# A two-layer encoder trunk on one core: spreading matmuls, roots and partial sums placed at other points of the output stages

## The chip, the cores and the metric

The kernel runs on one core of a Trainium2 chip. The metric is the device time of one execution in microseconds (us), the median of several executions. The engines are TensorE (PE in the rows, PEld its weight loads), VectorE (DVE), ScalarE (ACT), GpSimd (POOL) and SyncE (SP), which issues nearly all DMA transfers.

## The reference, cut to what matters

Two layers, 2048 tokens, width 1024, float32. Each layer ends in the same way, and only this end is touched:

```python
h = h + (o * jax.nn.silu(z)) @ w_out                       # "front" products
gate = jax.nn.sigmoid(rms_norm(h, ple_norm_g[i]) @ ple_w_gate[i])   # "back" products
h = h + (p[i] @ ple_w[i]) * gate
...
return rms_norm(h, final_norm_g)                           # after the second layer
```

`o` is the attention output before its division by the softmax denominator, `z` the gate path, and `p[i] @ ple_w[i]` is computed ahead and lies in DRAM (`ple`).

## The kernel before

All activations are kept transposed (features on the partitions, tokens along the row), 512 tokens to a group `tg` (four groups). Every float32 operand is cut into a high and a low part, so one 128x1024 by 1024x512 product is 24 matmuls (helper `mm3`, lines 290 to 292).

**Order.** `Plan` collects steps with a due time and emits them sorted; PE, ACT, DVE and POOL execute in exactly that order, each engine in its own queue. The order of the DMA issues on SP isn't bound to the plan: the compiler places them itself. Due times inside the output stage count in units in which one 512-column product has `UNIT` = 5.19; `u` below is such a unit (about 1.05 us), and `8U` is one group (41.52 u).

**The output stage** is class `Post`, scheduled once after the first layer (Post 0) and once after the second (Post 1, `final`), each with 32 front products, then 32 back products (in Post 1 the last group is two half groups of 256 columns, called 3 and 4).

- Front, group `tg`: `front` (8 blocks f), `add` the residual (DVE, L812), `x_square` (ACT, L827), `gather` (POOL, L833: partial sums of squares), `x_load` and `x_store` (SP, L804, L818) over a ring of three buffers `xrs`.
- Operands of the next group, c = 0 to 7: `o_load` (SP, L734 `of`, L737 `zt`; three buffer pairs `duos`), `o_spread` (one matmul, L771, that spreads the reciprocal denominators over 64 rows each), `o_gate` (DVE L778, then POOL L779), `o_cut` (ACT L216, DVE L218). Before them, once per group, `spread_load` (SP, L753) and `spread_cut` (ACT L761 twice, DVE L763).
- Sum of a group (`sums_at`): `sum_split` (ACT L216, DVE L218 into blkE), `sum_mm` (two matmuls, L266), `sum_copy`, `sum_out` and `root_in` (DMA out and in), `root` in three steps (DVE L236; ACT square root L240; DVE L244 to L249), `root_out` (DMA, L876, 512 separate floats to `rs`). `SUMS` holds their distances. `row_in` (DMA, L283) later broadcasts `rs` to all partitions; the row scales the back products.
- Back, group g: `h_load` (L887), `h_cut` (ACT L228, DVE L229) for the next group; `back`; `mixin` steps 0 to 4 (DVE L922, ACT L927 sigmoid, POOL L929 gate product, DVE L931, ACT L827); `gather`; `p_load` (L904), `h_store` (L936). In Post 1, `finish` (DVE L940) applies the final norm to a group after its `row_in`; the half groups take their root by `turn` (PE L950, DVE L956, ACT, DVE L249, PE L970) without DRAM, and the last one ends in `finish_last`.

The dense attention ahead of Post 1 ends with `recip` and `store_recip` of its last unit.

Of the kernel before, what the change touches and what calls it, by code (L numbers as in the profile page):

```python
# [18 lines left out]
D = 1024  # L19
T = 2048  # L20
NT = T // P
NC8 = D // P
TG = 512
NG = T // TG
# [8 lines left out]
STLAG, PSLAG = 1.5, 1.19  # L33
US = 1 / 1.3
UNIT = 5.19
PS_X, PS_EV, PS_ST, PS_SS, PS_H, PS_P, PS_HS, PS_SB = 2.17, 0.61, 2.06, 6.29, 1.2, 3, 0.68, 6.5
L_FIRST, L_PACE, L_CUT = -32, 2.6, (9.44, 10.74, 22.24, 26.4, 32.24)
L_US, PS_SL = -0.33, 6.5
A_W1 = ((0, 1), (1, 2), (2, 4), (4, 8))
PREP, PLE_LD = 3, 12  # L40
PS_O1 = 15.5
PS_WL, PS_OL, PS_OL2, PS_HL, PS_R1, PS_R2 = 4, 4, 3.72, 3.96, 2.57, 3
L_LD, L_UL, L_KR, L_VS, L_QS, L_NS = 4, 4, 3, 1.8, 1.8, 1.8
G_WL, G_UL, G_R, G_ST = 4.5, 4.5, 3.5, 2.2
D_S, D_S2 = 0.02, 0.05
D_K0, D_KP, D_KM, D_Q, D_R2, D_V = 0.64, 3.7, 9.5, 8, 27, 19
D_LAT, D_RR, D_W = 19, 20, 21
SUMS = (3, 4.2, 5, 7.5, 10.5, 10.7, 13, 14)
G_W, G_U = (-15.79, -9, 2, 8), -9.81
PL_SUM = (4.5, 5.8, 6.6, 8, 9.5, 10.6)  # L50
VLAG, GATHAT, ACCAT, DENAT, RECIPAT = 4.3, 1.3, 1.4, 8.4, 13.4
KLAG, RLAG, OLAG, DLAG, ILAG = 1, 0.8, 1, 0.8, 0.6
# [79 lines left out]
class Plan:  # L132
# [5 lines left out]
    def add(self, t, f, *args):  # L138
        self.steps.append((t, f, args))
# [537 lines left out]
class Post:  # L677
# [4 lines left out]
    def __init__(self, k, layer, spots, o_dram, rden, z_dram, w_out, resid, out, early):  # L682
        self.k, self.layer, self.final = k, layer, layer == 1
        self.o_dram, self.rden, self.z_dram, self.resid, self.out = o_dram, rden, z_dram, resid, out
        self.srcs = (w_out, k.a["ple_w_gate"][layer])
        w0, w1, self.ospots = spots["w0"], spots["w1"], spots["o"]
        self.wspots = w0, w1 + w0[:4]
        halves = [((blk, kb), (blk, kb + 2)) for spot in w0[4:] for blk, kb in spot]
        self.hspots = self.ospots[0], halves
        self.stages = k.fring(*((4,) * early + (0, 4) * 8))  # L690
        two, rows, baccs = ((36, 38, 40), (30, 32), (28, 34)) if self.final else ((30, 32, 34), (36, 38), (28, 40))
        self.ins = [[("F", kb) for kb in kbs] for kbs in ((8, 10, 12), two if self.final else (0, 2, 14))]
        self.duos = [[("F", kb) for kb in kbs] for kbs in ((8, 10), (12, two[0]), two[1:])]
        self.rdens = k.ring(*(("R", kb) for kb in (88, 90)) if self.final else (("Y", kb) for kb in (8, 10)))
        self.selspot = ("R", 92) if self.final else ("Y", 12)
        self.xrs, self.sqs, self.faccs, self.baccs = k.fring(18, 20, 22), k.fring(26), k.fring(24, 14), k.fring(*baccs)
        self.lasts = k.fring(4, 6)
        self.rows, self.gts, self.plts = k.fring(*rows), k.fring(18, 20, 22), k.fring(26, 14)
        self.spare = ("F", baccs[1])
        first = [("F", kb) for kb in (8, 10, 12, *two, 24, 16)]  # L700
        if self.final:
            self.hfs = first + [("Z", 2 * i) for i in range(16)] + first
        else:
            self.hfs = (first + [("F", kb) for kb in (0, 2, 4, 6)]) * 3
        self.mps, self.sums = k.banks(0, 7), k.banks(7, 8)
        self.w = [[None] * NC8, [None] * NC8]
        self.st = {}
        self.segs = [(0, 512), (512, 512), (1024, 512)] + ([(1536, 256), (1792, 256)] if self.final else [(1536, 512)])
        self.gate_g = k.gam[:, 2 + layer]
# [154 lines left out]

    def root(self, i, g, step):
        if step == 0:
            self.st["root"] = self.k.root_start(self.st["ss"], D, "p")
        elif step == 1:
            self.k.root_table(self.st["root"])
        else:  # L870
            out = self.k.rcol[:, 4 * g : 4 * g + 4] if i == 2 and not self.final else None
            self.st["r"] = self.k.root_end(self.st["root"], out)

    def root_out(self, i, g):
        dst = self.k.rs[self.slot(i)][self.span(i, g)].rearrange("(t p) -> p t", p=P)
        self.k.nc.sync.dma_start(dst, self.st["r"])  # L876

    def row_in(self, i, g):
        sp = self.span(i, g)
# [64 lines left out]
    def turn(self, g, step):  # L944

        k, nc = self.k, self.k.nc
        if step == 0:
            acc = self.st.pop(("acc", 2, g))
            self.st["s"] = self.sums.next()[:, : acc.shape[-1]]
            nc.tensor.matmul(self.st["s"], lhsT=fv(k.ones), rhs=acc, start=True, stop=True)  # L950
        elif step == 1:
            ps = self.st["s"]
            n = ps.shape[-1] // P
            ss, junk = k.small.tile("sp", 4)[:, :n], self.gts.tile([P, P])
            for i in range(n):
                nc.vector.tensor_tensor_reduce(  # L956
                    out=junk, in0=ps[:, i * P : (i + 1) * P], in1=k.ident, scale=1.0, scalar=0.0,
                    op0=ALU.mult, op1=ALU.add, accum_out=ss[:, i : i + 1],
                )
            self.st["root"] = k.root_start(ss, D, "p")  # L960
        elif step == 2:
            k.root_table(self.st["root"])
        elif step == 3:
            self.st["r"] = k.root_end(self.st["root"])
        elif step == 4:
            r = self.st["r"]
            n = r.shape[-1]
            ps = self.mps.next()[:, : n * P]
            for i in range(n):
                nc.tensor.transpose(ps[:, i * P : (i + 1) * P], r[:, i : i + 1].broadcast_to([P, P]), k.ident)  # L970
            self.st["rowp"] = ps
        else:
            row = self.lasts.tile([P, self.st["rowp"].shape[-1]])
            nc.scalar.copy(row, self.st["rowp"])
            self.st["row", 2, g] = row
# [31 lines left out]
    def schedule(self, plan, base, tables):  # L1007
# [5 lines left out]
        for tg in range(NG):  # L1013
            for f in range(NC8):
                t = (NC8 * tg + f) * UNIT
                te = t + UNIT + PS_EV
                add(t, self.front, tg, f)
                add(te - PS_X, self.x_load, tg, f)
                add(te, self.add, tg, f)
                add(te + 0.9, self.x_square, tg, f)  # L1020
                add(te + 1.6, self.gather, 1, tg, f)
                add(te + PS_ST, self.x_store, tg, f)
                if tg > 0:
                    to = NC8 * (tg - 1) * UNIT + (PS_O1 + 3.2 * f if tg == 1 else 4.7 * f + 4)
                    add(to - PS_OL2 - (4.2 if tg > 1 else 3.3), self.o_load, tg, f)
                    add(to - 0.6, self.o_spread, tg, f)
                    add(to, self.o_gate, tg, f, "both")
                    add(to + 1.9, self.o_cut, tg, f, "both")
                    if f == 0:
                        add(to - 7, self.spread_load, tg)  # L1030
                        add(to - 2, self.spread_cut, tg)
            self.sums_at(add, NC8 * (tg + 1) * UNIT + PS_SS, 1, tg)
        t = NG * NC8 * UNIT
        for tg in range(NG):
            tb = t + NC8 * tg * UNIT
            add(tb - (PS_R1 if tg < NG - 1 else PS_R2), self.row_in, 1, tg)
            for f in range(NC8):
                th = tb - NC8 * UNIT + (0.5 + 0.8 * f if tg == 0 else 1.2 + 0.75 * f) * UNIT + PS_H
                add(th - PS_HL, self.h_load, tg, f)
                add(th, self.h_cut, tg, f)  # L1040
        for g, (lo, n) in enumerate(self.segs):
            x, last = n / TG, self.final and g == len(self.segs) - 1
            unit = x * UNIT
            for f in range(NC8):
                te = t + unit + PS_EV
                add(t, self.back, g, f)
                add(te - PS_P, self.p_load, g, f)
                for i, dt in enumerate((0, 0.9, 1.7, 3.2, 4.1) if n == TG else (0, 0.55, 1, 1.9, 2.5)):
                    add(te + dt, self.mixin, g, f, i)
                add(te + (4.9 if n == TG else 3), self.gather, 2, g, f, "vector" if last else "gpsimd")  # L1050
                t += unit
                if not self.final:
                    add(te + 4.2 + PS_HS, self.h_store, g, f)
# [14 lines left out]
                        add(times[5] + 0.8 + f, self.finish, g, f)  # L1068
                        add(times[5] + 1.6 + f, self.h_store, g, f)
            if self.final and n == TG:  # L1070
                fin = t + PS_SB + 20
                add(fin - 3, self.row_in, 2, g)
                for f in range(NC8):
                    add(fin + 1.3 * x * f, self.finish, g, f)
                    add(fin + 1.3 * x * f + 1, self.h_store, g, f)
# [442 lines left out]
class Dense:  # L1518
# [212 lines left out]
    def schedule(self, plan, base):  # L1731

        nu = len(self.units)
        for u, (h, g) in enumerate(self.units):
# [16 lines left out]
            plan.add(t0 + NT + ACCAT, self.split_acc, u)  # L1751
            plan.add(t0 + NT + DENAT, self.density, u)
            plan.add(t0 + NT + DENAT + DLAG, self.spread, u)
            plan.add(t0 + NT + RECIPAT, self.recip, u)
            plan.add(t0 + NT + RECIPAT + ILAG, self.store_recip, u)
            if h % 2 == 1 and h + 1 < HEADS and g < 2:
                for i in range(2):
                    plan.add(t0 + KAT[i] + 0.5, self.k_mm, (h + 1) // 2, 2 * g + i)
# [66 lines left out]
```

## Time and profile before

| | us |
|---|---|
| three runs, median (lowest, highest) | 3672.93 (3672.21, 3678.47) |
| the profiled execution | 3679.53 |
| its span, first to last instruction | 3677.8 |
| mean granted TensorE clock, share of full | 0.985 |
| PE, DVE, ACT, POOL busy, share of the span | 97%, 65%, 62%, 54% |

In the profiled execution the front products of Post 0 begin at 837.55 and its back products at 1047.19; those of Post 1 begin at 3254.53 and 3454.12. A product of 24 matmuls without disturbance takes 5.44 us from start to start (2.88 us with 256 columns), a spreading matmul 0.23, and the two matmuls of a sum 0.45. In a time line, the bracket behind an instruction is the idle time of its engine just before it and what ended it. "Releasers" are inferred from semaphores.

### The profile page before, as it was taken

The numbers are of one execution on the slowest core, as the hardware profiler recorded it, in microseconds if no ns is written. First come the engines' busy times: TensorE is split into PE (matmuls) and PEld (weight loads), VectorE is DVE, ScalarE is ACT, GpSimd is POOL, SyncE is SP. The second block draws the span as 40 slices with busy tenths as digits, with TensorE's granted clock in tenths as the row PEclk, the third lists the DMA queues.
The fourth block names the chain that finished last, engine by engine and source line by source line (L and its number), as shares of the span: only waits on it lengthen the run. The fifth ranks groups of instructions, "written<-read, shape, count | busy, mean of one in ns | idle before, by whom it ended". The sixth has DMA issues, their size and how long they took to land. (4 is left out here: it accounts for less than half of the span.)

```text
span 3677.8 us, 52432 instructions
## 1 busy us (share of the span) xinstructions
PE 3551.2 (97%) x17118; PEld 2967.2 (81%) x17118; DVE 2404.9 (65%) x4539; ACT 2277.0 (62%) x4267; POOL 1973.3 (54%) x1564
## 2 busy tenths in 40 slices
PE   8999999999899899999999999999999999989997
PEld 6888888877787798899888888888888888867776
DVE  6111169995444444514989898989898989964445
ACT  6111279994233433422989898989898989952333
POOL 5331310033333432111989898989898989953243
PEclk9999999999999999999999999999999999999998
DMA  5332378876654676654111212121212121066533
GB/s 189 134 118 89 106 208 203 199 193 200 165 142 133 162 220 220 224 163 131 36 51 35 54 36 59 35 58 36 57 36 58 36 63 36 26 193 178 173 97 106
DMA packets 380080, 428.18 MB, mean 116 GB/s; under 512 B 46287, under 2 KB 233167, under 8 KB 379102
## 3 DMA queue, kind: packets, MB, share of 16 engines
q1 hardware_dynamic: 360798, 390.75, 38.8%
q10 hardware_dynamic: 19008, 34.09, 2.5%
q8 instruction: 134, 2.20, 0.3%
q14 instruction: 140, 1.15, 0.1%
HBM read 251.65 MB, written 156.17 MB: 111 GB/s over the span
## 5 line engine op out<-in xcount | busy, mean ns | idle before, releaser
L1648 POOL TENSOR_TENSOR blkR<-blkF,blkX 128x512 fp32r<-128x512 f32 x1024 | 1351.6, 1333 | 177.8 <-PE ps L1638 51.7
L1609 DVE TENSOR_REDUCE blkF<-ps 128x1 f32<-128x512 f32 x1024 | 700.5, 684 | 77.4 <-PE ps L1605 41.6
L1640 ACT ACTIVATE blkF<-ps 128x512 f32<-128x512 f32 x1024 | 611.4, 597 | 100.1 <-PE ps L1638 51.1
L1641 ACT CAST blkX<-blkF 128x512 fp32r<-128x512 f32 x1024 | 635.5, 621 | 32.8
L1658 DVE TENSOR_TENSOR ps<-ps,blkF 128x512 f32<-128x512 f32 x896 | 615.5, 687 | 0.7
L1669 PE MATMUL ps<-blkR 128*128 128x512 f32 x1024 | 405.4, 396 | 1.1 <-POOL blkR L1648 1.1
L1668 PE MATMUL ps<-blkX,blkR 128*128 128x512 f32 x1024 | 405.2, 396 | 0.0
L290 PE MATMUL ps<-blkR 128*128 128x512 f32 (+2 forms) x888 | 341.2, 384 | 5.6 <-ACT blkR L216 5.4
L291 PE MATMUL ps<-blkR 128*128 128x512 f32 (+2 forms) x888 | 339.2, 382 | 0.6 <-DVE blkR L218 0.6
L292 PE MATMUL ps<-blkR 128*128 128x512 f32 (+2 forms) x888 | 338.9, 382 | 0.3 <-DVE blkR L218 0.3
L833 POOL TENSOR_TENSOR blkF<-blkF 128x512 f32<-128x512 f32 (+1 forms) x112 | 145.8, 1302 | 247.0 <-ACT blkF L827 236.8
L363 DVE TENSOR_TENSOR blkF<-ps,blkF 128x512 f32<-128x512 f32 x72 | 49.5, 691 | 301.4 <-PE ps L292 296.4
L218 POOL TENSOR_TENSOR blkR<-blkF,blkR 128x1024 fp32r<-128x1024 f32 (+1 forms) x39 | 73.5, 1889 | 305.6 <-ACT blkR L216 278.2
L1669 PEld LDWEIGHTS ps<-blkR 128*128 128x128 f32 x1024 | 194.7, 190 | 47.0 <-POOL blkR L1648 2.4
L1668 PEld LDWEIGHTS ps<-blkX,blkR 128*128 128x128 f32 x1024 | 194.9, 190 | 44.2
L827 ACT ACTIVATE blkF<-blkF 128x512 f32<-128x512 f32 (+1 forms) x120 | 72.2, 602 | 221.9 <-DVE blkF L812 112.3
L290 PEld LDWEIGHTS ps<-blkR 128*128 128x128 f32 x888 | 171.0, 193 | 36.9 <-ACT blkR L216 6.2
L292 PEld LDWEIGHTS ps<-blkR 128*128 128x128 f32 x888 | 170.5, 192 | 31.6 <-DVE blkR L218 1.0
L291 PEld LDWEIGHTS ps<-blkR 128*128 128x128 f32 x888 | 170.8, 192 | 29.7 <-DVE blkR L218 0.9
L223 DVE TENSOR_TENSOR blkR<-ps,blkR 128x512 fp32r<-128x512 f32 (+2 forms) x232 | 143.5, 625 | 48.9 <-ACT blkR L222 48.7
L1636 PE MATMUL ps<-blkZ 96*128 96x512 f32 x384 | 155.0, 404 | 7.8 <-ACT blkF L1640 7.8
L290 PE MATMUL ps<-blkR,blkX 128*128 128x512 f32 (+1 forms) x384 | 149.6, 390 | 11.9 <-ACT blkX L216 9.2
(272 smaller groups left out, 9030.2 us busy)
## 6 DMA issues: line engine op xcount, KB each, us to landing
h<-blkF SPq DMA_DIRECT2D x96, 256.0 KB
blkF<-h SPq DMA_DIRECT2D x80, 256.0 KB
a_qs<-blkF ACTq DMA_DIRECT2D x64, 256.0 KB
ple<-blkF SPq DMA_DIRECT2D x64, 256.0 KB
blkF<-h SPq DMA_DIRECT2D x32, 512.0 KB
b_v<-blkX SPq DMA_DIRECT2D x32, 512.0 KB
b_q<-blkX SPq DMA_DIRECT2D x64, 256.0 KB
blkZ<-b_q SPq DMA_DIRECT2D x64, 256.0 KB
```

What stands on the lines that cost most here:

```text
L290: mm(out, lhsT=lh, rhs=rh, start=(first and i == 0), stop=False)
L291: mm(out, lhsT=lh, rhs=rl, start=False, stop=False)
L292: mm(out, lhsT=ll, rhs=rh, start=False, stop=(last and i == n - 1))
L833: getattr(self.k.nc, eng).tensor_tensor(out=acc, in0=acc, in1=sq, op=ALU.add)
L1609: nc.vector.tensor_reduce(out=mm[:, qt, kc : kc + 1], in_=ps, axis=AX.X, op=ALU.max)
L1636: nc.tensor.matmul(sp, lhsT=kl[:, kt_], rhs=qh[0:96, :], start=True, stop=False)
L1640: nc.scalar.activation(pe, sp, AF.Exp, scale=SCALE_B)
L1641: nc.scalar.copy(ph, pe)
L1648: nc.gpsimd.tensor_tensor(out=pl, in0=pe, in1=fv(ph), op=ALU.subtract)
L1658: nc.vector.tensor_tensor(out=st["acc"], in0=prev, in1=st[kt][0], op=ALU.add)
L1668: nc.tensor.matmul(st["o"], lhsT=v, rhs=ph, start=(kt == 0), stop=False)
L1669: nc.tensor.matmul(st["o"], lhsT=v, rhs=pl, start=False, stop=(kt == NT - 1))
```

## The change

Only due times, one ring and some names of intermediate results change; no instruction is added or dropped.

```diff
-PS_X, PS_EV, PS_ST, PS_SS, PS_H, PS_P, PS_HS, PS_SB = 2.17, 0.61, 2.06, 6.29, 1.2, 3, 0.68, 6.5
+PS_X, PS_EV, PS_ST, PS_SS, PS_H, PS_P, PS_HS, PS_SB = 4.4, 0.61, 2.06, 9.3, 1.2, 3, 0.68, 10
...
-PS_O1 = 15.5
-SUMS = (3, 4.2, 5, 7.5, 10.5, 10.7, 13, 14)
+SUMS = (3, 4.2, 5, 7.5, 16.5, 16.7, 19, 20)
+CUTAT, GATHB = (2.7, 1.9), 7.05
...
-        self.xrs, self.sqs, self.faccs, self.baccs = k.fring(18, 20, 22), k.fring(26), k.fring(24, 14), k.fring(*baccs)
+        self.xrs, self.sqs, self.faccs, self.baccs = k.fring(18, 20, 22, rows[1]), k.fring(26), k.fring(24, 14), k.fring(*baccs)
...
                 if tg > 0:
-                    to = NC8 * (tg - 1) * UNIT + (PS_O1 + 3.2 * f if tg == 1 else 4.7 * f + 4)
-                    add(to - PS_OL2 - (4.2 if tg > 1 else 3.3), self.o_load, tg, f)
-                    add(to - 0.6, self.o_spread, tg, f)
+                    before = 3 + f // 2 if tg == 1 else NC8 * (tg - 1) + f
+                    to = (3 + f / 2 if tg == 1 else before) * UNIT + 0.6
+                    add(to - PS_OL2 - (6 if tg > 1 else 1.3), self.o_load, tg, f)
+                    add(before * UNIT - 0.01, self.o_spread, tg, f)
                     add(to, self.o_gate, tg, f, "both")
-                    add(to + 1.9, self.o_cut, tg, f, "both")
+                    add(to + CUTAT[tg > 1], self.o_cut, tg, f, "both")
                     if f == 0:
-                        add(to - 7, self.spread_load, tg)
-                        add(to - 2, self.spread_cut, tg)
-            self.sums_at(add, NC8 * (tg + 1) * UNIT + PS_SS, 1, tg)
+                        add(to - 9, self.spread_load, tg)
+                        add(to - 4.5, self.spread_cut, tg)
+            self.sums_at(add, NC8 * (tg + 1) * UNIT + (PS_SS if tg < NG - 1 else 6.29), 1, tg)
...
-                add(th - PS_HL, self.h_load, tg, f)
+                add(th - PS_HL - (0 if tg == 0 else 2), self.h_load, tg, f)
...
-                add(te + (4.9 if n == TG else 3), self.gather, 2, g, f, "vector" if last else "gpsimd")
+                if last or g == len(self.segs) - 1 and f == NC8 - 1:
+                    dt = 4.9 if n == TG else 3
+                else:
+                    dt = GATHB if n == TG else 3.7
+                add(te + dt, self.gather, 2, g, f, "vector" if last else "gpsimd")
...
-                fin = t + PS_SB + 20
+                fin = t + PS_SB + 26
...
-            plan.add(t0 + NT + RECIPAT, self.recip, u)
-            plan.add(t0 + NT + RECIPAT + ILAG, self.store_recip, u)
+            tr = t0 + NT + RECIPAT + (4 if u == nu - 1 else 0)
+            plan.add(tr, self.recip, u)
+            plan.add(tr + ILAG, self.store_recip, u)
```

`PS_SS` is the due time of `sum_split` after a front group, `PS_SB` after a back group; the last group of Post 0 and the half groups keep theirs. `rows[1]` is the second of the two buffers that `row_in` of the fronts' sums uses in turn. The intermediate results `root` and `r` are now kept by sum and group, since two roots may be under way.

## Rows read from the trace of the kernel before

**Rows 1.** The page, busy time of each engine, share of the span, instructions:

```profile
PE 3551.2 (97%) x17118; PEld 2967.2 (81%) x17118; DVE 2404.9 (65%) x4539; ACT 2277.0 (62%) x4267; POOL 1973.3 (54%) x1564
```

**Rows 2.** PE by stretch, Post 0: start:end, length, PE busy (matmuls), granted clock, DMA:

```profile
1064.02:1085.78 21.76, 21.76 (x98) 1.00 0.37 86
887.46:904.94 17.48, 13.51 (x50) 0.90 0.66 193
939.68:959.33 19.65, 13.96 (x51) 0.83 0.70 208
994.06:1019.99 25.93, 20.29 (x76) 0.87 0.71 214
1096.66:1115.72 19.06, 14.60 (x51) 0.82 0.54 168
...
1197.33:1214.56 17.23, 14.75 (x52) 0.80 0.59 168
```

**Rows 3.** The same for Post 1:

```profile
3304.69:3321.88 17.19, 13.42 (x51) 0.90 0.63 189
3356.61:3372.07 15.46, 13.00 (x50) 0.89 0.66 204
3406.80:3426.93 20.13, 17.40 (x76) 1.00 0.67 195
...
3544.11:3571.25 27.14, 21.02 (x75) 0.87 0.65 204
3598.45:3609.02 10.57, 7.77 (x50) 0.84 0.57 203
3611.90:3621.66 9.76, 8.23 (x52) 0.83 0.19 54
3639.36:3655.38 16.02, 8.64 (x52) 0.69 0.46 147
3664.15:3677.80 13.65, 1.55 (x6) 0.69 0.23 77
```

**Rows 4.** PE's waits: total us, times, longest; two of Post 0, one of Post 1:

```profile
PE ps L266 <- ACT blkE L216: 9.7, 3, 4.5
PE ps L771 <- DVE blkY L763: 5.0, 2, 2.6
...
PE ps L950 <- DVE blkF L833: 3.2, 1, 3.2
```

**Rows 5.** SP's own waits, same columns: Post 0, then Post 1:

```profile
SPq L804 <- DMA h<-blkF: 101.7, 29, 11.1
...
SPq L283 <- DMA rs<-blkF: 41.9, 5, 9.9
```

**Rows 6.** Time line of SP, Post 0, before the third front group: start, us, issue:

```profile
924.38 0.38 SPq L876 DMA_DIRECT2D rs<-blkF  x1
...
934.70 0.32 SPq L283 DMA_DIRECT2D blkF<-rs  x1
937.08 0.33 SPq L804 DMA_DIRECT2D blkF<-in_c_xT  x1
```

**Rows 7.** Time line of DVE, Post 1, the first `finish` of group 0:

```profile
3540.06 0.75 DVE L940 SCALAR_TENSOR_TENSOR blkF<-blkF,gam 128x512 f32<-128x512 f32 x1 [9.64 <-DMA blkF<-rs]
```

**Rows 8.** Time line of DVE, Post 0, the last cuts before the second front group:

```profile
889.20 0.69 DVE L218 TENSOR_TENSOR blkZ<-blkF,blkZ 128x512 fp32r<-128x512 f32 x1 [2.05 <-ACT blkZ L216]
...
893.14 1.09 DVE L218 TENSOR_TENSOR blkZ<-blkF,blkZ 128x512 fp32r<-128x512 f32 x1 [2.05 <-ACT blkZ L216]
...
896.74 0.70 DVE L763 TENSOR_TENSOR blkY<-blkF,blkY 16x512 fp32r<-16x512 f32 x1 [1.90 <-ACT blkY L761]
```

**Rows 9.** Time line of POOL, Post 0: a sum among those cuts, the last sums of back group 0:

```profile
892.41 1.27 POOL L833 TENSOR_TENSOR blkF<-blkF 128x512 f32<-128x512 f32 x1
...
1100.70 1.30 POOL L833 TENSOR_TENSOR blkF<-blkF 128x512 f32<-128x512 f32 x1 [1.53 <-ACT blkF L827]
...
1104.75 1.26 POOL L833 TENSOR_TENSOR blkF<-blkF 128x512 f32<-128x512 f32 x1 [1.53 <-ACT blkF L827]
```

More of the change, by code (lines that the diff above doesn't have):

```diff
@@ L866, in root @@
         if step == 0:
-            self.st["root"] = self.k.root_start(self.st["ss"], D, "p")
+            self.st["root", i, g] = self.k.root_start(self.st["ss"], D, "p")
         elif step == 1:
-            self.k.root_table(self.st["root"])
+            self.k.root_table(self.st["root", i, g])
         else:
             out = self.k.rcol[:, 4 * g : 4 * g + 4] if i == 2 and not self.final else None
-            self.st["r"] = self.k.root_end(self.st["root"], out)
+            self.st["r", i, g] = self.k.root_end(self.st["root", i, g], out)
     def root_out(self, i, g):
         dst = self.k.rs[self.slot(i)][self.span(i, g)].rearrange("(t p) -> p t", p=P)
-        self.k.nc.sync.dma_start(dst, self.st["r"])
+        self.k.nc.sync.dma_start(dst, self.st["r", i, g])
     def row_in(self, i, g):
@@ L959, in turn @@
                 )
-            self.st["root"] = k.root_start(ss, D, "p")
+            self.st["root", 2, g] = k.root_start(ss, D, "p")
         elif step == 2:
-            k.root_table(self.st["root"])
+            k.root_table(self.st["root", 2, g])
         elif step == 3:
-            self.st["r"] = k.root_end(self.st["root"])
+            self.st["r", 2, g] = k.root_end(self.st["root", 2, g])
         elif step == 4:
-            r = self.st["r"]
+            r = self.st["r", 2, g]
             n = r.shape[-1]
```

## The prediction

> **What bounds the kernel now.** The page comes first: PE is busy 97% of the span [rows 1], so only PE's pauses, and the slow clock behind them, can be won. Next comes PE by stretch. The undisturbed stretch holds four products in 21.76 us at full clock, 5.44 each [rows 2]; half-width products (2.88), spreading matmuls (0.23) and sums (0.45) are set off the same way. In every other stretch of rows 2 and 3, length less this work is lost time:
>
> - Post 0, first products of front groups 1 to 3: 17.48 - 11.11 = 6.4; 19.65 - 11.11 = 8.5; 25.93 - 16.77 = 9.2 (this one holds a sum too). Together 24.1.
> - Post 0, the sums of back groups 0 to 2, which PE meets after two products of the next group: 19.06 - 11.33 = 7.7 and 17.23 - 11.33 = 5.9 are the first and the last of three, with 5.0 between. Together 18.6.
> - Post 1, fronts: 6.1, 4.4 and 3.4, together 13.9. Backs: 27.14 - 16.77 = 10.4, 10.57 - 5.76 = 4.8, 9.76 - 6.21 = 3.5, together 18.7. The root of the first half group: 16.02 - 6.1 = 9.9. The tail after the last product is 13.65.
>
> [...]
>
> Who ends the pauses stands in PE's waits: `spread_cut` (L763), the split of a sum (L216 into blkE), and the last half group's sum on DVE [rows 4]. Behind these I see two causes. First, SP. x_load waits for the landing of the store before it, 101.7 us in 29 waits in Post 0 [rows 5]; and `row_in`, due only at the end of the fronts, is issued right behind `root_out` and holds SP from 925 to 934.70, because the 512 floats take 10.3 us from issue to landing [rows 6]; a 256 KB store issued among them lands late too (the longest of those waits, 11.1 [rows 5]). Second, in-order DVE: it stands 2.05 us before each `o_cut` while POOL and ACT work, so a block c takes 893.14 - 889.20 = 3.94 us, and `spread_cut` is queued behind the eighth [rows 8].
>
> **The change part by part.** Terms are made against the profiled 3679.5 us (span 3677.8 and 1.7 around it); this execution lies 6.6 above the median, and the sum is taken off the median.
>
> *Spreads, gates, cuts.* For group 1 the blocks now come in pairs per product, 2.6 units apart instead of 3.2, and the cut 2.7 behind its gate, so gate c+1 stands before cut c on DVE and covers the 2.05 us [rows 8]. DVE's work per product is two gates, two cuts and a residual add, each like the 0.69 of a cut alone [rows 8], and often a weight cut of twice the width (estimate 1.2): 4.6 us of the 5.9 that a product with two spreads takes. The last cut is due at 37.0 instead of 39.8, behind the add of product 6. Nothing is queued behind the eighth cut but `spread_cut`, due at 37.6 instead of 43.5, now ahead of the squares of product 6. But the spread that needs it also moves ahead by one product. From product 6's end I count add 0.7, cut 0.7, L763 0.7 and about 1.5 of queueing, 3.6 us, against the 5.4 of product 7. Left of 6.4 (and 6.1 in Post 1): 0 to 6, I take 3.
>
> *Groups 2 and 3.* `spread_cut` again 5.9 units earlier, the spread one product. `root_out` moves from 20.3 to 29.3 units after the group, so that the 10.3 us in which SP stands [rows 6] begin after the eighth block's loads (due 27.2). The loads of the next group's second block come behind the block, but have some 10 units of lead. The fourth x buffer is a row buffer: the second group's `row_in` can no longer be issued early, and x loads have a product more lead. It must wait for what lay there (an attention store), bounded by one store's landing, 0 to 6 us on SP, covered by three free buffers. Left of 8.5 + 9.2: 2 each at the groups' starts and 2 at the sum, whose split is 3 units and its matmul one product (5.44) later. Post 0's fronts: 24.1 - 9 = 15.1 gained. Post 1, same edits with smaller pauses: 3 + 1.5 + 1.5 left, 7.9 gained.
>
> *Back sums.* The split is due at 10 instead of 6.5, the matmuls at 13 instead of 9.5, behind one more product: 5.44 us more cover for pauses of up to 4.5 [rows 4]. Against it, `gather` of product 7 now stands behind the next group's first gate product on POOL, and the split behind that product's square on ACT. In Post 0's group 0 the last gather starts 4.05 us after the one before it, and ends at 1106.01, 14.8 us after the group's last product (1096.66 - 5.44 = 1091.22) [rows 2, 9]; one more such loop, less the 1.3 us of gather that leaves it, and the split gives 14.8 + 2.75 + 0.7 = 18.2 at worst; a loop without gather is 2.75, which three products of lag win back to about 15. PE arrives at 16.3. Left 3 + 1.5 + 1.5 of 18.6: 12.6 gained. If the cover isn't enough, each sum costs as before.
>
> *Post 1, backs.* Here `finish` waits for its row: DVE stands 9.64 us [rows 7], with `row_in` on SP up to 9.9 [rows 5]. The distances from `root_out` to `row_in` (3) and `finish` (6) are as before, so DVE will stand as long; but from unit 36 of the next group on instead of 26.5, behind all cuts of h (the last is due at 34.7) instead of ahead of three. So the 4.8 and about 4.7 of the 10.4, both waits for those cuts, go. What is late next are the sums: the gate products of blocks 6 and 7 wait behind `finish`. Left 3 + 2 + 3: 18.7 - 8 = 10.7 gained.
>
> *Root of the half group and tail.* `finish` of group 2 now comes behind that root, so the 9.9 goes. It is given back: DVE stands until some 25.6 us after the half group's start (unit 36 is at 16.0, plus 9.6), where the products end after 23.5. Then eight `finish` at about 0.67 (one alone takes 0.75 [rows 7]) and some 5.5 us of other DVE work remain, to 36.6. The tail, in which PE waits 3.2 for DVE today [rows 4], grows by 9.9, and by 2 for eight stores close to the end: -2 in all. The later dense reciprocal, h loads two units earlier and the new names cost nothing on PE's path; the loads issue when buffers free.
>
> *Sum:* 15.1 + 12.6 + 7.9 + 10.7 - 2 = 44.3. From 3672.9: **3628.6 us**.
>
> *A rule against the change.* The cut that took 0.69 us at 889.20 took 1.09 at 893.14, while POOL's sum ran from 892.41 for 1.27 us [rows 8, 9]. The Trainium skill ("SBUF — State Buffer", "Who interferes with whom") says why: a DVE instruction with two SBUF inputs and a GpSimd instruction that reads SBUF share a read interface, and the later one waits until the other has finished. The trace agrees. Cuts that now run beside the next gate's POOL product would meet this eight times per group; it is a rival below.
>
> **The rivals.** (1) *SP stays the pace.* Each x load still stands right behind a store, whose landing it waits for: 3.5 us on average [rows 5]. Against: a product more lead. Fronts then keep 38.0; only backs and tail count: 12.6 + 10.7 - 2 = 21.3, 3651.6.
> (2) *Every pause goes*, only the tail's 11.9 stays: 85.2 - 11.9 = 73.3, 3599.6.
> (3) *POOL's reads hold the cuts of group 1.* Eight cuts, each by up to a whole POOL product of 1.29: 10.3 us on DVE against 3 of margin, a pause of 7 and 2 of slow clock in place of 3, in both stages: 12 less, 3640.6.
> (4) *Slower: the spread overtakes its cut.* PE now meets the first spread of a group one product earlier, 5.67 us. If eighth cut and `spread_cut` don't come earlier (loads late, DVE behind), PE stands there 5.7 longer, in three groups of two stages: 34; less the 21.3 of the backs, 12.7 slower, 3685.6. It decides from the point where L763 ends after the product ahead of the group. Today it ends 2.4 us after the group's first product [rows 4, 8].
> (5) *Nothing:* SP's order is the compiler's, and waits change place; 3672.9 within 0.2%.
>
> **How the numbers follow.** Forecast 0.47 (3612 to 3645), (1) 0.20, (2) 0.09, (3) 0.06, (4) 0.09, (5) 0.09. A difference under 0.2% (7.3 us) can't be told from none. Faster: 0.82, same 0.09, slower 0.09. The range 3604 to 3668 leaves out (4), half of (2) and two thirds of (5): 0.20.
>
> **What would show it.** Right: no wait of PE for L763 over 1 us; the sum's matmuls after three products, with L216 pauses gone in Post 0; L940 still standing over 8 us, later in its group; the wait at L970 under 3 us, and a tail of over 20 us. Wrong: L804 on SP waiting as long while front groups still take over 50 us each (rival 1); L763 ending after the product (rival 4); a sum ready later than 16.3 us after its group, which would leave the backs where they are.

## The result, and the profile after

| | before | after |
|---|---|---|
| median of four runs each, us | 3675.70 | 3634.22 (3631.72 to 3636.30) |
| ratio, 95% interval | | 0.9886 (0.9874 to 0.9898) |
| the profiled execution, us | 3679.53 | 3632.4 |
| its span, us | 3677.8 | 3630.6 |

41.5 us between the medians, 47.2 between the two spans. The forecast was 44.3 less, 3628.6, within 3604 to 3668. The page of the kernel after, engines' busy time (for before: [rows 1]):

```profile
PE 3523.7 (97%) x17118; PEld 2951.4 (81%) x17118; DVE 2458.6 (68%) x4539; ACT 2278.3 (63%) x4267; POOL 1988.0 (55%) x1564
```

PE does the same 17118 matmuls in 27.5 us less busy time, because it runs less at the low clock: in Post 0's fronts the granted clock is 1.00 instead of 0.96, and PE's busy time 185.4 us instead of 193.9. Where the span went is read from PE by stage. The next view is PE by stretch in the kernel after, columns as in [rows 2], with the busy time of PEld, DVE, ACT and POOL between PE's and the clock: Post 0's fronts and backs, the entry of the latents (the first steps of the second layer's attention, right behind Post 0), Post 1's fronts, its backs, and the tail.

```profile
835.00:1021.25 186.25, 185.43 (x822) 152.84 (x823) 106.28 (x142) 68.59 (x111) 73.28 (x54) 1.00 0.73 210
1021.25:1197.96 176.71, 176.49 (x778) 145.56 (x777) 96.44 (x116) 74.75 (x112) 75.31 (x56) 1.00 0.57 148
1197.96:1233.71 35.75, 18.82 (x104) 17.45 (x103) 21.04 (x26) 14.80 (x26) 17.25 (x15) 0.81 0.62 145
3218.44:3405.27 186.83, 186.10 (x807) 153.38 (x808) 105.12 (x133) 66.25 (x101) 75.60 (x56) 0.98 0.71 201
3405.27:3604.41 199.14, 185.02 (x973) 159.75 (x971) 113.91 (x159) 74.58 (x124) 82.31 (x66) 0.97 0.37 103
3604.41:3630.61 26.20, 2.18 (x7) 0.86 (x5) 16.10 (x40) 5.61 (x13) 4.48 (x5) 0.57 0.54 185
```

In Post 0 PE now pauses 0.8 us in the fronts and 0.2 in the backs, at full clock throughout. Nearly all that is left lies in the entry of the latents and in Post 1's backs and tail.

The same stages of several kernels, worked out from the starts of the same matmuls in each trace (one profiled execution each; the entry here reaches ten latent products far). The stretch ahead of Post 0, which is outside these stages, already differs by up to 5 us between these executions, so a difference of one or two us in one cell is no finding:

| us | before | after | e1 | e2 | e3 | e5 | e7 | e9 | e10 | e11 | e12 |
|---|---|---|---|---|---|---|---|---|---|---|---|
| Post 0 fronts | 209.6 | 186.3 | 197.9 | 188.1 | 190.7 | 186.3 | 187.9 | 186.3 | 204.3 | 186.3 | 186.3 |
| Post 0 backs | 194.6 | 176.7 | 180.9 | 207.6 | 183.0 | 176.3 | 177.4 | 176.6 | 177.7 | 176.7 | 176.5 |
| latents' entry | 56.0 | 64.2 | 63.9 | 55.5 | 63.3 | 55.0 | 55.4 | 63.8 | 56.3 | 58.2 | 54.9 |
| Post 1 fronts | 199.6 | 186.8 | 192.1 | 188.2 | 187.2 | 186.9 | 185.6 | 186.8 | 204.5 | 186.8 | 186.7 |
| Post 1 backs | 209.9 | 199.1 | 201.0 | 220.3 | 202.1 | 191.7 | 190.6 | 199.5 | 186.5 | 201.0 | 179.9 |
| tail | 13.7 | 26.2 | 24.1 | 19.1 | 24.3 | 24.4 | 20.0 | 25.2 | 22.7 | 24.9 | 18.0 |

(Backs of Post 1 end at PE's last product matmul.) From before to after: 23.4 + 17.9 - 8.2 + 12.8 + 10.8 - 12.5, and 3.0 outside these stages, 2.5 of them ahead of Post 0: 47.2.

PE's waits in the kernel after (total us, times, longest; for before: [rows 4]) say who ends the pauses: one of Post 0's backs, one of the latents' entry, three of Post 1's backs and tail.

```profile
PE ps L266 <- DVE blkE L218: 0.2, 1, 0.2
...
PE ps L290 <- ACT blkR L216: 12.1, 1, 12.1
...
PE ps L950 <- DVE blkF L833: 14.1, 1, 14.1
PE ps L266 <- ACT blkE L216: 11.1, 2, 5.9
...
PE ps L950 <- POOL blkF L833: 2.1, 1, 2.1
```

No wait for L763 is left, and in Post 0's backs 0.2 us of waits for a sum. The 12.1 at the entry was 4.0 before.

**The entry.** Time lines of SP and ACT there, then the engines by stretch, columns as above:

```profile
1200.43 0.37 SPq L876 DMA_DIRECT2D rs<-rcol  x1
1200.90 0.45 SPq L1121 DMA_DIRECT2D blkF<-in_c_wq  x1
...
1212.99 0.62 ACT L216 CAST blkY<-blkF 128x512 fp32r<-128x512 f32 x1 [10.21 <-DMA blkF<-in_c_wq]
```

```profile
1204.00:1210.00 6.00, 3.36 (x22) 3.09 (x21) 1.88 (x2) 0.00 (x0) 1.33 (x1) 1.00 0.65 36
```

The root of group 2, now due 9.5 units later than before, sends its 512 floats 0.47 us ahead of a query weight. The weight can be cut 12.1 us after its issue (1212.99 - 1200.90); meanwhile the DMA engines are 65% busy at 36 GB/s, and the next cut for PE stands behind this one on ACT.

**The tail.** Time lines of SP, DVE and POOL behind the root of group 2:

```profile
3591.52 0.37 SPq L876 DMA_DIRECT2D rs<-blkF  x1
3600.24 0.32 SPq L283 DMA_DIRECT2D blkF<-rs  x1
3600.66 0.38 SPq L904 DMA_DIRECT2D blkF<-ple  x1
...
3606.01 0.75 DVE L940 SCALAR_TENSOR_TENSOR blkZ<-blkZ,gam,blkF 128x512 f32<-128x512 f32 x1 [7.58 <-DMA blkF<-rs]
...
3606.45 0.90 POOL L929 TENSOR_TENSOR blkF<-blkF 128x256 f32<-128x256 f32 x1 [10.33 <-DMA blkF<-ple]
```

Two engines come free within half a microsecond of each other: DVE, which stood for the row, and POOL, which stood for a block of `ple` whose load SP issued only behind `row_in`, and that one 8.7 us after the floats.

### The profile page after: what moved, and what is told of

It is laid out like the page before. It is cut to its first block, busy times and chain, and to the rows that moved or that the text cites. A ratio compares the mean times of both kernels' runs of the same rounds, so it can differ in the third digit from the quotient of the medians.

```text
span 3630.6 us, 52438 instructions
## 1 busy us (share of the span) xinstructions
PE 3523.7 (97%) x17118; PEld 2951.4 (81%) x17118; DVE 2458.6 (68%) x4539; ACT 2278.3 (63%) x4267; POOL 1988.0 (55%) x1564
## 4 chain that ended last, share of the span: by engine, by line
PE 83%; DVE 6%; DMA 4%; ACT 3%; issue 2%; POOL 1%; SPq 0%; ACTq 0%; DVEq 0%; POOLq 0%
PE ps L292 12%; PE ps L290 12%; PE ps L291 12%; PE ps L1610 7%; PE ps L1643 6%; PE ps L1673 6%; PE ps L1641 6%; PE ps L1674 6%; PE ps L1642 6%; PE ps L597 2%; DVE blkF L931 1%; DMA blkF<-ple 1%; PE ps L612 1%; PE ps L552 1%; PE ps L553 1%
## 5 line engine op out<-in xcount | busy, mean ns | idle before, releaser
L1674 PEld LDWEIGHTS ps<-blkR 128*128 128x128 f32 x1024 | 194.7, 190 | 47.0 <-POOL blkR L1653 2.6
L929 POOL TENSOR_TENSOR blkF<-blkF 128x512 f32<-128x512 f32 (+1 forms) x70 | 85.2, 1217 | 236.0 <-ACT blkF L927 209.9
L833 POOL TENSOR_TENSOR blkF<-blkF 128x512 f32<-128x512 f32 (+1 forms) x112 | 160.7, 1435 | 97.4 <-ACT blkF L827 91.1
L290 PEld LDWEIGHTS ps<-blkR 128*128 128x128 f32 x888 | 168.3, 189 | 34.5 <-ACT blkR L216 3.1
L292 PEld LDWEIGHTS ps<-blkR 128*128 128x128 f32 x888 | 168.0, 189 | 31.6 <-DVE blkR L218 1.2
L291 PEld LDWEIGHTS ps<-blkR 128*128 128x128 f32 x888 | 168.2, 189 | 28.4
```

The lines of the kernel that those rows point to most:

```text
L290: mm(out, lhsT=lh, rhs=rh, start=(first and i == 0), stop=False)
L291: mm(out, lhsT=lh, rhs=rl, start=False, stop=False)
L292: mm(out, lhsT=ll, rhs=rh, start=False, stop=(last and i == n - 1))
L1674: nc.tensor.matmul(st["o"], lhsT=v, rhs=pl, start=False, stop=(kt == NT - 1))
```

## The experiments

Two theories at first. A: the front pauses went because spreads and cuts stand elsewhere. B: they went because SP is no longer held by the roots' floats and `row_in`.

### e1: spreads, gates and cuts put back

```diff
-                    before = 3 + f // 2 if tg == 1 else NC8 * (tg - 1) + f
-                    to = (3 + f / 2 if tg == 1 else before) * UNIT + 0.6
+                    to = NC8 * (tg - 1) * UNIT + (15.5 + 3.2 * f if tg == 1 else 4.7 * f + 4)
...                  o_load, o_spread, o_cut, spread_load, spread_cut likewise
```

> The changed kernel with the due times of o_load, o_spread, o_gate, o_cut, spread_load and spread_cut put back to those of the kernel before; the fourth x buffer, the later roots and the later sums stay. Theory A (the placing of the spreading matmuls and cuts took the front pauses): the 24 us of Post 0's fronts and the 14 of Post 1's come back, 3655 to 3672 us against 3634, and PE waits for L763 again. Theory B (SP took them: the later root_out and the fourth x buffer let x loads through): the pauses stay away, 3634 to 3645.

Measured: 0.9970 (0.9959 to 0.9981) of the kernel before. Post 0's fronts 197.9 us. PE's waits there, and then in Post 1's fronts:

```profile
PE ps L771 <- DVE blkY L763: 4.1, 2, 2.6
...
PE ps L771 <- DVE blkR L763: 2.6, 1, 2.6
```

Of the 23.4 us won in Post 0's fronts 11.6 come back, of Post 1's 12.8 it is 5.3. Theory A holds for half of it; the other half stays without the spreads' new places. What stays in e1 is not only ring and roots, but also the earlier x loads (`PS_X`) and the later front sums (`PS_SS`), which no run takes back alone.

### e2: roots, rows and finish put back

```diff
-SUMS = (3, 4.2, 5, 7.5, 16.5, 16.7, 19, 20)
+SUMS = (3, 4.2, 5, 7.5, 10.5, 10.7, 13, 14)
-                fin = t + PS_SB + 26
+                fin = t + PS_SB + 20
```

> The changed kernel with SUMS and the due time of finish put back, so that the roots, root_out, row_in and finish come 6 units earlier; spreads and sums stay changed. Theory A: the front pauses stay away. Ahead of the latents 8 us are won back (the 512 floats are written before the first query weights are loaded, not just ahead of them), Post 1's two waits for h cuts cost 9.5 again, the half group's root 9, and the tail gives 12 back: 3628 to 3640. Theory B: root_out stands among the x loads again, and half or more of the 38 us of both stages' fronts come back: 3648 to 3668.

Measured: 1.0012 (1.0002 to 1.0021). Neither theory expected where: the fronts stay short (188.1 and 188.2), the entry, counted from its first product, recovers, but Post 0's backs take 207.6 us, 13 more than before the change and 31 more than after it; Post 1's take 21 more. Time lines of SP, ACT and DVE in the first group of Post 0's backs:

```profile
1046.92 0.37 SPq L862 DMA_DIRECT2D blkF<-sq  x1
...
1047.75 1.28 ACT L240 ACT_TABLE_LOAD   x1
1052.59 0.21 ACT L240 ACTIVATE blkF<-blkF 128x4 f32<-128x4 f32 x1 [3.56 <-DVE blkF L236]
...
1052.39 0.17 DVE L236 TENSOR_SCALAR blkF<-blkF 128x4 f32<-128x4 f32 x1 [3.27 <-DMA blkF<-sq]
```

The sums make a trip through DRAM, and `root` is due only 3 units behind their load (L862), which is issued at 1046.92; this is the fronts' last sum, which is due as before. The matmuls of the back sums now stand behind a third product on PE, due 13 units after the group where the product ends at 15.6 (before: 9.5 and 10.4), so these sums are sent later against the root's due time; two of their roots stand 1.3 us each. In the view, DVE stands at L236 for the load, ACT at its square root for DVE, and the sigmoids and `h` cuts of the running group are queued behind both. The kernel before had that wait too in the backs of Post 0 (DVE's and ACT's waits); DVE's is longer in total there than in e2 (5.8 us in three waits):

```profile
DVE blkF L236 <- DMA blkF<-sq: 8.3, 4, 2.7
...
ACT blkF L240 <- DVE blkF L236: 4.2, 3, 2.8
```

So a theory C: the pauses of Post 0's backs were this standing, and the later root removed them, not the later sum.

The same move has a second path, which theory C leaves out: the root's 512 floats go out among the loads of `h`. Time lines of SP and ACT, in the kernel before ahead of the second of the three pauses, then in e2 at the end of the backs:

```profile
1125.26 0.37 SPq L876 DMA_DIRECT2D rs<-rcol  x1
1126.65 0.32 SPq L887 DMA_DIRECT2D blkF<-h  x1
...
1138.70 0.72 ACT L228 ACTIVATE blkR<-blkF,gam 128x512 fp32r<-128x512 f32 x1 [4.02 <-DMA blkF<-h]
```

```profile
1215.41 0.38 SPq L876 DMA_DIRECT2D rs<-rcol  x1
1216.84 0.37 SPq L1135 DMA_DIRECT2D blkF<-h  x1
...
1227.77 1.04 ACT L216 CAST blkR<-blkF 128x1024 fp32r<-128x1024 f32 x1 [8.94 <-DMA blkF<-h]
```

In the kernel before the load behind the floats is cut 12.05 us after its issue, and ACT stood for `h` twice ahead of each pause, 16.7 us in six waits in all. In e2 it is 13.2 in four, and the load shown holds the latents' first product: PE waits 8.0 us for it, which count as the end of the backs and are more than half of the 13. So the floats, sent earlier, missed the weights and met this load.

### e3: three x buffers

```diff
-k.fring(18, 20, 22, rows[1])
+k.fring(18, 20, 22)
```

> The changed kernel with the ring of three x buffers; all due times stay changed. Theory A: nothing on PE's path, 3632 to 3640. Theory B: row_in is issued early again and x loads have one product less of lead, so that part of the front pauses comes back: 3644 to 3660.

Measured: 0.9943 (0.9926 to 0.9960), span 13.2 longer than after. Post 0's fronts lose 4.5; 6.3 more are lost at the start of its backs, where an x load stood for its store. SP's wait for the row in the fronts is back, and in the backs DVE stands for a residual:

```profile
SPq L283 <- DMA rs<-blkF: 6.0, 2, 5.9
...
DVE blkF L812 <- DMA blkF<-in_c_xT: 8.8, 1, 8.8
```

In the kernel after SP doesn't wait at L283 in the fronts. The buffer is worth this much in Post 0, as theory B says, though mostly behind the fronts; Post 1's fronts lose 0.4.

### e4 and e5: the back sums put back, the roots kept late

```diff
-PS_HS, PS_SB = ..., 0.68, 10
+PS_HS, PS_SB = ..., 0.68, 6.5
-CUTAT, GATHB = (2.7, 1.9), 7.05
+CUTAT, GATHB = (2.7, 1.9), 4.9
...
+            dt += 3.5 if i == 2 and g < 3 and n > 3 else 0     # root steps and root_out only
...
-                fin = t + PS_SB + 26
+                fin = t + PS_SB + 29.5
```

In e4 the shift began two steps earlier, at `sum_out`: the row of a sum was overwritten by a gate product before it was sent, so its roots are not those of the sums, though all the work is there. e5 has the right order.

> The changed kernel with the split of the back sums, their matmuls and GpSimd's partial sums put back (split 6.5 units after the group, gather 4.9 behind the product); roots and finish keep their changed places. If the later sums took the pauses of Post 0's backs: 18 us come back there, and some 2 in Post 1, 3648 to 3656. If the pauses went because the roots no longer stand between (rival): 3632 to 3640.

> The changed kernel (ratio to the kernel before 0.9886) with the back sums put back whole: split 6.5 units after the group, gather 4.9 behind the product, matmuls, copy and both transfers at their old distances; only the three steps of the root, root_out, row_in and finish keep their changed places. If the later roots took the pauses of Post 0's backs, as the trace of the kernel before shows DVE standing at L236 for the 512 sums there (8.3 us in four waits): no pause returns, and the ratio is 0.985 to 0.988. If the later sums were needed, as the prediction counted: 18 us return in Post 0, 0.993 to 0.995.

Measured: e4 0.9861 (0.9846 to 0.9876), e5 0.9858 (0.9842 to 0.9875). No pause returns in Post 0: in e5's backs there PE waits for no sum and DVE not at L236; they take 176.3 us. The later place of the sums is worth nothing in Post 0, and elsewhere it costs: e5 is faster than the changed kernel as measured again in e9 (0.9898) by 0.0040 of 3667, or 14.7 us (against its first ratio, 0.9886, it is 0.0028, or 10 us), with an entry of 55.0 us instead of 63.8 and Post 1's backs of 191.7 instead of 199.5 (e9). At the entry the sum is ready earlier, and the floats leave at 1192.20, 5.4 us ahead of the latents' first product, instead of 2.5 us behind it. So the part of the title on partial sums was a loss; e5 puts split, matmuls and GpSimd's sums back together and doesn't say which of them.

### e10: the roots alone

The kernel before, with `SUMS` and `fin` of the change and the names kept by sum and group; nothing else.

> The kernel before with one part of the change alone: root steps, root_out, row_in and finish 6 units later (the names kept by sum and group, as they must be); spreads, x ring, sums, gather and all else as before. Theory C (the pauses of Post 0's backs are DVE standing for the sums' way through DRAM): those 18 us go, Post 1's h cuts and half group gain 19 and its tail gives 12 back, the latents lose 8, the fronts gain 0 to 19: ratio 0.990 to 0.996. Rival (the roots are worth nothing in Post 0, as the prediction counted them there): 0.998 to 1.001.

Measured: 0.9940 (0.9928 to 0.9953). Post 0's backs take 177.7 us, so 16.9 of the 17.9 come with the roots alone. PE's longest wait there:

```profile
PE ps L266 <- ACT blkE L216: 0.6, 1, 0.6
```

So theory C is shown in one half: the later root takes the pauses of Post 0's backs away (e5, e10), and the later sum is not needed. By which path is not shown, since no run moves the root's standing or its floats alone, and the traces speak more for the floats. ACT's sigmoids (L927) around the square roots ahead of the three pauses lie 9.6, 6.5 and 7.1 us apart in the kernel before and 6.7, 6.5 and 6.5 in e10: past the first group hardly a change. Around the longest waits for `h` they lie 10.0, 10.2 and 9.9 us apart before, 5.3, 4.2 and 6.4 in e10, and these waits fall from 16.7 us to 5.8 (e5: 2.2).

The entry is as before (56.3), Post 1's backs and tail together gain 14.4 (the whole change: -1.7). Post 1's fronts get 4.9 us longer: PE waits 4.3 us there for the split of a sum, 2.1 before; what holds that split is not settled.

### e6 and e11: the floats out of the weights' way

```diff
+            if not self.final and i == 2 and g == 2 and n == 7:   # e6: root_out alone; e11: n > 3
+                dt += 28                                          # e11: 25
```

> The changed kernel with one step moved: root_out of Post 0's group 2 comes 28 units later, behind the query weights of the latents. If its 512 floats hold the weight loads issued behind them (ACT waited 10.2 us for a weight): PE's 12.1 us wait there falls to 4, and the ratio from 0.9886 to 0.9862 to 0.9868. Rival, the latents are late because ACT, DVE and POOL are behind with group 3: the wait stays, 0.988 to 0.989.

> The changed kernel with the three root steps and root_out of Post 0's group 2 25 units later, so that the 512 floats are written after the latents' query weights have landed (moving root_out alone left its issue where it was). If those floats hold the weights: the wait of ACT for in_c_wq there goes from 10 us to under 4, PE's from 12.1 to under 5, and the ratio is 0.002 below the changed kernel's of this call. Rival (the latents are late by the work of group 3): the same ratio.

e6: 0.9901 (0.9886 to 0.9916), and no test: SP issued the floats at 1202.00, right ahead of a weight as ever, since the DMA order isn't bound to the plan and the data was ready. e11: 0.9892 (0.9879 to 0.9906), beside 0.9898 for the changed kernel (e9). ACT's wait for the weights and PE's at the entry, first in the changed kernel (e9), then in e11:

```profile
ACT blkY L216 <- DMA blkF<-in_c_wq: 9.7, 1, 9.7
PE ps L290 <- ACT blkR L216: 10.0, 1, 10.0
```

```profile
ACT blkY L216 <- DMA blkF<-in_c_wq: 3.7, 3, 2.7
PE ps L290 <- ACT blkR L216: 1.3, 1, 1.3
```

The cause is shown: without the floats among them the weights come in time. The gain is not there: of 8.7 us won in the first three products 3.1 go in the next seven, among whose loads the floats are now sent (argued, not tested), 2.3 in the attention behind them and 1.5 in Post 1's backs, which the edit doesn't touch; two cells of this size are within what single executions differ by. The ratios can't be told apart.

### e7 and e8: who holds the tail

```diff
 # e7, on e5
+            if self.final and i == 2 and g == 2 and n > 3:
+                dt = (12.5, 12.7, 15, 16)[n - 4]
 # e8, on the changed kernel
+                    tf = fin + 1.3 * x * f + (10 if g == 2 else 0)    # finish, and h_store 1 later
```

> e5_sums_early with one more edit: in Post 1 the root of group 2 comes 7.5 units earlier (12.5 behind the split), its row_in and finish stay. Theory X+Y (in the tail DVE and SP both stand for the row of group 2, 7.6 and 8.3 us): the row is there when finish is due, the tail is 8 to 14 us shorter than in e5, ratio 0.003 lower. Rival: the root again stands in the half group's way, as before the change (9.9 us lost there): same as e5 or slower.

> The changed kernel with finish and h_store of Post 1's group 2 10 units later; row_in stays. Theory X (DVE, standing at L940 for the row, holds the last half group's mixins): the tail is 4 to 9 us shorter, 0.9862 to 0.9876. Theory Y (SP, standing at L283 for the 512 floats, holds the last loads of ple, for which POOL waited 10.3 us): the mixins are as late, and eight finishes then follow them: the same or up to 6 us longer, 0.9886 to 0.990.

Measured: e7 0.9846 (0.9831 to 0.9861), tail 20.0 against 24.4 in e5; e8 0.9911 (0.9897 to 0.9926). Waits of POOL and PE in the tails, e7 then e8:

```profile
POOL blkF L929 <- DMA blkF<-ple: 8.3, 2, 4.9
PE ps L950 <- DVE blkF L833: 9.0, 1, 9.0
```

```profile
POOL blkF L929 <- DMA blkF<-ple: 9.7, 1, 9.7
PE ps L950 <- DVE blkF L833: 9.8, 1, 9.8
```

In e8 DVE no longer stands for the row, and PE's last wait falls from 14.1 to 9.8; POOL still stands 9.7 for `ple`, and the end doesn't move, because eight `finish` now follow. X alone falls (the ratio lies a little above Y's range). In e7 the row is earlier and both waits are shorter, but the gain is 4.5, not 8 to 14: SP still stands for the floats ahead of loads of `ple`.

### e9 and e12: the mark, and a version that takes the findings together

```diff
+            if self.final and i == 2 and n > 3:
+                dt = (12.5, 12.7, 15, 16)[n - 4]          # e12, on e5; and Post 0's group 2 as in e11
-        self.nc.sync.dma_start(dst, self.rs[i]...
+        (self.nc.scalar if by_act else self.nc.sync).dma_start(dst, self.rs[i]...   # by_act: back groups
-                add(fin - 3, self.row_in, 2, g)
+                add(fin - 1.5, self.row_in, 2, g)
+                fin += 4
```

> The changed kernel itself, beside the next three on the same chip: 0.9886 of the kernel before again, within 0.987 to 0.990. Every theory expects the same; it is the mark for the other runs of this call.

> e5_sums_early with, in Post 1, all roots of back groups at 12.5 behind the split (4 later than that today would be 16.5 plus 3.5), their row_in issued from ACT's queue at 34.5 units after the group and finish at 40, and with the root of Post 0's group 2 moved as in e11. If SP standing for the row (8 us, loads of ple behind it) and DVE standing for it make the losses left in Post 1: no wait of DVE for rs over 2 us, no wait of POOL for ple over 4, sums' waits under 3, tail under 30: ratio 0.977 to 0.982. Rival (ACT now stands for the 512 floats, with sigmoids and squares behind it): 0.984 or more.

e9: 0.9898 (0.9882 to 0.9913). e12: 0.9809 (0.9795 to 0.9822), 3597.3 us beside 3630.2 for e9 and 3667.7 for the kernel before. Waits of PE, DVE and POOL in e12's Post 1, backs and tail:

```profile
PE ps L950 <- DVE blkF L833: 4.4, 1, 4.4
...
DVE blkF L236 <- DMA blkF<-sq: 2.2, 1, 2.2
POOL blkF L929 <- DMA blkF<-ple: 5.6, 2, 3.6
```

No wait for a sum (L266), none of DVE for a row, 18.0 us of tail. Post 1's backs fall to 179.9 us. e12 beats both kernels; it changes four things at once, so it doesn't say what each is worth.

The Trainium skill ("DMA: Bandwidth & Descriptors", "Issuing engines are not separate DMA queues") says that issuing from several engines at once saves only the sequencer's time to initiate a DMA, which is usually small. The trace agrees on that time, 0.32 us for the row's issue in the tail of the kernel after. What was not small is the wait ahead of the issue, of which the sentence doesn't speak: SP stood 8.3 us for that row, with loads behind it. What the row's move to ACT's queue is worth by itself, no run shows.

## Why the prediction was right or wrong

**Fronts: right in sign, too small.** Forecast 15.1 and 7.9, measured 23.4 and 12.8. The step that failed is the term for what is left: 9 and 6 us were put down for `spread_cut` and queueing, and under 1 us is left in Post 0. The working itself was close, and the margin is thin. Time line of DVE, Post 0, ahead of the second front group, and one of POOL's products beside its second cut:

```profile
875.35 1.10 DVE L218 TENSOR_TENSOR blkZ<-blkF,blkZ 128x512 fp32r<-128x512 f32 x1
...
878.30 1.44 DVE L218 TENSOR_TENSOR blkZ<-blkF,blkZ 128x512 fp32r<-128x512 f32 x1 [0.64 <-ACT blkZ L216]
...
884.44 0.68 DVE L763 TENSOR_TENSOR blkY<-blkF,blkY 16x512 fp32r<-16x512 f32 x1 [0.47 <-ACT blkY L761]
885.97 0.69 DVE L778 TENSOR_TENSOR blkF<-ps,blkF 128x512 f32<-128x512 f32 x1 [0.84 <-PE ps L771]
...
877.90 1.29 POOL L779 TENSOR_TENSOR blkF<-blkF 128x512 f32<-128x512 f32 x1 [0.28 <-DMA blkF<-a_o]
```

L763 ends at 885.12, and PE starts the spread that needs it at 885.54: 0.42 us early, where the forecast had 1.8. Rival 4 was that near, and e1, e2 and e3, whose L763 comes later, do wait for it. These two cuts took 1.10 and 1.44 us instead of the 0.69 of a cut alone [rows 8], the second while POOL's product ran until 879.19. So rival 3's mechanism is there, as the rule of the Trainium skill named in the prediction ("SBUF — State Buffer", "Who interferes with whom") has it. How much of the margin it took is not shown: the engine that L763 stood for last is ACT (L761), whose own last cut had stood 2.77 us for a POOL product.

**Rival 1, SP as the pace,** did not come: SP still waits for stores in Post 0's fronts, 79.1 us in 24 waits against 98.4 in 28 in the same stage before, and no product waits for it:

```profile
SPq L804 <- DMA h<-blkF: 79.1, 24, 8.9
...
DVE blkF L236 <- DMA blkF<-sq: 14.5, 3, 7.8
```

The second line, DVE in the same fronts, shows that even 14.5 us at L236 cost nothing there; that gates and cuts have a product of lead is the likely reason, not a tested one. But half of the gain, which the forecast had given to the spreads, lies in the rest of the change (e1). Of that, the ring is worth 4.5 us in Post 0 and 0.4 in Post 1 (e3); the later roots alone win 5.3 in Post 0 and lose 4.9 in Post 1 (e10), and taking them back costs 1.8 and 1.4 (e2). How much the x loads and the front sums bear is not shown.

**Rival 2, every pause goes,** came true in Post 0 alone, where 41.3 of the 42.7 us of lost time went (24.1 and 18.6 in the prediction).

**Back sums of Post 0: a gain as forecast, for a wrong reason.** Forecast 12.6, measured 17.9. The step that failed is one more product of cover for the sum: e5 and e10 have the sums at their old place and no pause over 0.6 us, e2 has the cover and keeps its pauses. That the term came out near was luck: the root steps, to which the prediction gave no part in these pauses, were moved in the same change. What I had not read were two waits in the trace of before, DVE's at L236, 8.3 us, and ACT's for `h`, 16.7 us; I had taken PE's releaser, the split into blkE [rows 4], without asking what it was queued behind. The floats had been priced in the fronts alone.

**Latents' entry: not foreseen, 8.2 us lost.** The floats' 10.3 us [rows 6] were in the working, and their effect on a store among them; what is loaded next to the new place of `root_out` was followed only to the end of Post 0.

**Post 1's backs: 20.6 forecast (10.7 and the half group's 9.9), 10.8 measured.** The pauses for `h` cuts went and the half group's root costs 0.9 us, as worked out. What was mis-sized is what is left: 18.7 + 9.9 - 10.8 = 17.8 us where 8 were put down; 11.1 of it are the two sums that PE still waits for, 5.1 and 5.9, and part of the rest is slow clock (granted 0.97 in this stage). L940 stood 3.4, 5.1 and 7.6 us, not over 8. In e5, with the sums early, these backs are 7.8 shorter than in e9; in e10, with the sums and all but the roots as before, they take 186.5.

**Tail: 11.9 forecast, 12.5 measured,** right in size and half in mechanism: besides DVE, SP holds it (e8).

**The sum** came out close by luck, because misses cancelled: 13 and 5 us more from fronts and Post 0's backs, 10 and 8 less from Post 1's backs and the entry.

## What to carry to other kernels

Behind a releaser that PE's waits name, ask what that instruction was queued behind on its own engine, and go on to the DMA that it ends at. Where two such waits move together, as here DVE's for a sum and ACT's for `h`, compare the gaps around each before naming one of them. When a small scattered write is moved, list the loads issued next to its new place, in the following stage too. A change made of several moves should be taken apart even when it wins: here one part, the back sums' new place, cost 10 to 15 us, and the gain of another was credited to it.

## What the runs showed of the hardware

512 separate floats (2 KB) on their way made a 256 KB load issued 0.47 us behind them usable only after 12.1 us, at 36 GB/s over the DMA engines; in e11, without them, no such load kept ACT waiting for over 2.7 us. In the kernel before, a 256 KB load of `h` issued 1.39 us behind such floats was cut 12.05 us after its issue. An issue that alone was moved in the plan by 28 units did not move on SP (e6: 1202.00, 2.6 us behind the latents' first product, as in e9).
